# One-hot rows of the dense gates: compares on Vector and GpSimd against products of index bits on TensorE

## The chip, the cores and the metric

The kernel runs on one core of one Trainium2 chip. The metric is the device time of one launch in microseconds (us); lower is better. The engines are named as the profile names them: PE is TensorE (PEld its weight loads), DVE is VectorE, ACT is ScalarE, POOL is GpSimd and SP the queue that issues most DMAs.

## The reference, cut to what matters

The model has two layers. Each ends in an expert layer (PEER) over 16384 single-neuron experts, numbered by a pair (i, j) of 0 to 127 each:

```python
        q = (xt @ w_q).reshape(n, PEER_HEADS, 2, PEER_DHALF)
        s = jnp.einsum('nhpd,hpkd->nhpk', q, keys).astype(jnp.float32)
        sv, si = lax.top_k(s, PEER_TOPK)
        cand = sv[:, :, 0, :, None] + sv[:, :, 1, None, :]
        cidx = si[:, :, 0, :, None] * PEER_NKEYS + si[:, :, 1, None, :]
        cs, ci = lax.top_k(cand.reshape(n, PEER_HEADS, -1), PEER_TOPK)
        eidx = jnp.take_along_axis(cidx.reshape(n, PEER_HEADS, -1), ci, axis=-1)
        gate = jax.nn.softmax(cs, axis=-1)
        a = jnp.einsum('nd,nhkd->nhk', xt, u[eidx]).astype(jnp.float32)
        w = (gate * jax.nn.gelu(a, approximate=False)).astype(xt.dtype)
        return jnp.einsum('nhk,nhkd->nd', w, v[eidx])
```

There are 8 heads; each keeps its 16 best i, its 16 best j and of their sums the 16 best. So every token has 128 selected experts, each with i, j and a gate.

## The kernel before, in words

The even mixer, the first expert layer, the odd mixer and the second expert layer follow one another. In an expert layer the last 128 of the 512 latent tokens (in the first layer the 256 context tokens too) fetch their experts' rows one by one (`gather`, L998 to L1024). For the first 384 tokens, three blocks of 128, all 16384 experts are computed densely (`dense_u`, `dense_w`, `dense_v`), and a dense matrix of gates, [i, token] for each j, holds zero wherever an expert was not selected. This matrix is what the change is about.

`peer` first opens a routing stage (`route`): `scores` (L872 and the lines before it) forms the scores and the top 16 of both key sets, `select` (L936 to L989) finds a block's 128 pairs: i in `fi` (L978), j in `fj` (L969), gates in `dgt` (L989), with a token on each partition. As soon as a block's two halves are selected, `gate_build` makes its gates, while the selections of the later blocks still run. Its tiles come out of the pool of the routing stage; `alloc` hands out five buffers of 128x1024 that `select` uses.

`gate_build` before (L1044 to L1093), for a block:
- PE transposes i, j and gates (L1055), so that the 128 selected experts of a token lie on the partitions. DVE splits an index into its upper 3 and lower 4 bits (L1056 to L1059).
- The block is cut into 8 chunks of 16 tokens. For a chunk DVE compares the upper bits with 8 values and the lower bits with 16 (four `is_equal`, L1070, tiles `gup` and `glow`), and POOL multiplies the gates into one of the lower tables (L1073).
- For each four tokens of a chunk, and for i and for j, one multiply (L1084) makes the one-hot rows `ghot`, 128x512, as upper times lower. So a chunk has eight multiplies; `GENG` gives five of eight to DVE and three to POOL. Six `ghot` buffers turn.
- For each token PE multiplies the one-hot rows of i by those of j (weighted with the gate) to a 128x128 matrix (L1090, tile `gps`; the trace has two instructions for one such product). ACT copies eight tokens at a time, reordered, to `gch` (L1092), and a chunk goes to DRAM (`gd`, L1093).

After the routing stage the dense stage loads these gates (`dG`, L1139) and runs 128 steps. Beside the gate work, the routing stage already computes the first products of 18 (first layer) or 27 (second) of the 128 steps (L1112 with `whi`, `wlo`, split on ACT at L185 and on DVE or POOL at L188, loaded through SP at L182), so that PE is not idle.

PSUM is full in the routing stage: two buffers `pj`, two of two banks `big` (`gps` among them) and two of one bank `po` (used here for the transposes at L1055 and for the scores).

The order on each engine is laid down when the program is built: a planner goes through simulated time, and an engine is given work that is ready and has its buffers; what the program issues first goes first, unless `later` or `issue_after` says otherwise. On the chip each engine then keeps that order, and so does the SP queue.

Of the kernel before, what the change touches and what calls it, by code (L numbers as in the profile page):

```python
# [60 lines left out]
def _cst_layout():  # L61
    off = 0
    for name, n in (("ident", 128), ("ones", 128), ("perm", 128), ("mf", 128), ("mb", 128),
                    ("iota", 128), ("start", 16), ("cos", 512), ("sin", 512)):
        CST[name] = (off, n)
        off += n
    return off
# [5 lines left out]
def constants():  # L73
# [27 lines left out]
    put("start", np.array(starts)[None, :])  # L101
    return c


class Kern:
    def __init__(self, ctx, tc, a, dbg=None):
# [8 lines left out]
        self.wcnt, self.wlo, self.ghot = 0, WL1, 0  # L115
# [12 lines left out]
        self.yd = self.dr.tile([2, D, 768], F32, name="yd")  # L128

# [11 lines left out]
    def mixing(self):  # L141
        """pools of the parts between the expert layers"""
# [13 lines left out]
    def later(self, offset=1 << 20):  # L156
        """what is issued inside gives way to what is issued up to `offset` later"""
# [20 lines left out]
    def weight(self, src, shape):  # L178
        """src: DRAM AP of `shape` ([128, k, n], 1024 elements a row); returns (hi, lo)."""
# [11 lines left out]
    def wT(self, w, c0):  # L191
        """columns c0..c0+128 of the weights w as [128 k, 8, 128]."""
# [725 lines left out]
    def select(self, l, V, I, out, half, alloc):  # L918
# [17 lines left out]
        if fi is None:  # L936
            fi, fj = W(4, 16), W(4, 16)
# [584 lines left out]
```

## Time and profile before

| | us |
|---|---|
| median of 3 runs (lowest, highest) | 4348.12 (4344.39, 4353.43) |
| span of the profiled execution, first to last instruction | 4350.6 |
| PE busy | 3739.3 (86%) |
| DVE busy | 3715.8 (85%) |
| POOL busy | 2683.4 (62%) |
| ACT busy | 1603.3 (37%) |

The profiled execution has no other time of its own than its span, which already lies within the three runs. A page of the profile gives busy time by engine, the chain of work that ended last and the costliest groups; the views of the trace cut that to a stretch, a line or a tile. The routing stages with their gate work lie at about 1080 to 1515 us (first layer) and 2930 to 3390 us (second).

### The profile page before, as it was taken

To read this page: it belongs to the slowest core of one execution; us is meant where nothing else is said; L and a number is where in the kernel's file an instruction comes from. 1 tells how busy PE (TensorE), PEld (TensorE's weight loads), DVE (VectorE), ACT (ScalarE), POOL (GpSimd) and SP (SyncE) were. 2 spreads that over 40 slices of the span, in tenths; PEclk is the share of its full clock that TensorE was granted. 3 is DMA by queue.
4 is the path that set the end of the run, shared out by engine and by line. 5 is a ranking of instruction groups with operands and counts; after the bars stand their busy time and mean duration, and the time that the engine had idled before them with its cause. 6 is when DMAs were issued, how large, how long until landed. Compare 5 with 4: busy or idle time off the path is not lost.

```text
span 4350.6 us, 58785 instructions
## 1 busy us (share of the span) xinstructions
PE 3739.3 (86%) x20576; PEld 3297.7 (76%) x20576; DVE 3715.8 (85%) x6089; ACT 1603.3 (37%) x2676; POOL 2683.4 (62%) x1886
## 2 busy tenths in 40 slices
PE   7977666756687699999999968899886999999999
PEld 5776654445567689988889857787875899999987
DVE  6479989979999998898989989747999887777788
ACT  4433433412115533333333325443245433333333
POOL 3146777656656677777878667112577676666664
PEclk9998888878798999999999989999989999999999
DMA  5554888788742499999899988423234987887878
GB/s 192 187 185 158 276 284 280 263 308 317 241 135 109 184 337 336 332 320 327 318 331 335 341 301 290 160 84 125 94 126 168 321 309 272 285 287 269 288 264 313
DMA packets 382487, 1093.10 MB, mean 251 GB/s; under 512 B 32671, under 2 KB 134375, under 8 KB 376046
## 3 DMA queue, kind: packets, MB, share of 16 engines
q0 software_dynamic: 147456, 536.94, 34.8%
q1 hardware_dynamic: 224942, 491.58, 32.9%
q10 hardware_dynamic: 9792, 60.82, 3.4%
q8 instruction: 162, 2.65, 0.2%
q14 instruction: 135, 1.11, 0.1%
HBM read 1020.96 MB, written 68.26 MB: 250 GB/s over the span
## 4 chain that ended last, share of the span: by engine, by line
PE 40%; DVE 25%; issue 15%; DMA 11%; POOL 7%; ACT 2%; SPq 0%; POOLq 0%; DVEq 0%; ACTq 0%
PE dacc L1161 17%; PE dA L1112 14%; POOL uv L998 4%; DVE ghot L1084 4%; DMA uv<-in_pr_u_dram,ix 3%; DMA draw<-in_uT_dram 3%; DVE junkv L1011 3%; DMA uv<-in_pr_v_dram,ix 2%; PE ops L214 1%; DVE wlo L188 1%; DVE pacc L1024 1%; PE pqps L204 1%; DVE sel L916 1%; DVE gup L1070 1%; DVE sel L913 1%
## 5 line engine op out<-in xcount | busy, mean ns | idle before, releaser
L1161 PE MATMUL dacc<-dhi,dw 128*128 128x512 f32 x3072 | 989.1, 392 | 3.4 <-ACT dw L1154 1.8
L998 POOL DMA_INDIRECT uv<-in_pr_v_dram,ix x512 | 685.6, 1339 | 405.0 <-DVE pacc L1024 297.6
L998 POOL DMA_INDIRECT uv<-in_pr_u_dram,ix x512 | 685.2, 1338 | 373.6 <-DVE pa L1011 204.3
L1011 DVE CUSTOM_DVE_ANT_0 junkv<-uv,x 128x1024 bf16<-128x1024 f32 x512 | 734.7, 1435 | 39.5 <-DMA uv<-in_pr_u_dram,ix 35.5
L1024 DVE SCALAR_TENSOR_TENSOR pacc<-uv,pw,pacc 128x1024 f32<-128x1024 f32 x508 | 705.1, 1388 | 26.9 <-DMA uv<-in_pr_v_dram,ix 23.0
L1161 PEld LDWEIGHTS dacc<-dhi,dw 128*128 128x128 f32 x3072 | 579.9, 189 | 120.7 <-ACT dw L1154 2.1
L1101 ACT CAST dhi<-draw 128x1024 fp32r<-128x1024 f32 x467 | 489.2, 1050 | 463.6 <-DMA draw<-in_uT_dram 165.9
L1161 PE MATMUL dacc<-dlo,dw 128*128 128x512 f32 x1536 | 604.4, 394 | 11.1 <-DVE dlo L1102 11.0
L1102 POOL TENSOR_TENSOR dlo<-draw,dhi 128x1024 fp32r<-128x1024 f32 x210 | 545.5, 2598 | 95.6 <-ACT dhi L1101 91.9
L188 POOL TENSOR_TENSOR wlo<-wraw,whi 128x1024 fp32r<-128x1024 f32 x111 | 280.0, 2523 | 426.0 <-ACT whi L185 282.1
L1151 DVE TENSOR_TENSOR dz<-dz,dG 128x384 f32<-128x384 f32 x256 | 402.4, 1585 | 89.9 <-ACT dz L1121 88.5
L1154 ACT CAST dw<-dz 128x384 fp32r<-128x384 f32 x256 | 131.4, 513 | 690.8 <-PE dacc L1161 669.8
L1102 DVE TENSOR_TENSOR dlo<-draw,dhi 128x1024 fp32r<-128x1024 f32 x257 | 336.1, 1308 | 27.3 <-ACT dhi L1101 18.1
L185 ACT CAST whi<-wraw 128x1024 fp32r<-128x1024 f32 x195 | 204.3, 1049 | 416.6 <-PE pqps L204 101.5
L1112 PE MATMUL dA<-xth,dhi 128*128 128x384 f32 x1688 | 334.8, 340 | 10.1 <-ACT dhi L1101 6.9
L1161 PEld LDWEIGHTS dacc<-dlo,dw 128*128 128x128 f32 x1536 | 289.8, 189 | 70.1 <-DVE dlo L1102 13.3
L1112 PE MATMUL dA<-xtl,dhi 128*128 128x384 f32 x1688 | 327.4, 335 | 0.0
L1112 PEld LDWEIGHTS dA<-xth,dhi 128*128 128x128 f32 x1688 | 305.1, 189 | 28.5 <-ACT dhi L1101 7.8
L1112 PE MATMUL dA<-xth,dlo 128*128 128x384 f32 x1688 | 326.7, 334 | 0.0
L1090 PE MATMUL gps<-ghot 128*128 128x128 f32 x1536 | 231.8, 307 | 104.5 <-DVE ghot L1084 80.2
L1090 PEld LDWEIGHTS gps<-ghot 128*128 128x128 f32 x1536 | 211.2, 216 | 126.3 <-issue 84.4
L1112 PEld LDWEIGHTS dA<-xtl,dhi 128*128 128x128 f32 x1688 | 296.7, 188 | 0.0
(379 smaller groups left out, 6836.6 us busy)
## 6 DMA issues: line engine op xcount, KB each, us to landing
draw<-in_pr_v_dram SPq DMA_DIRECT2D x256, 512.0 KB
draw<-in_uT_dram SPq DMA_DIRECT2D x211, 512.0 KB
wraw<-in_wb_dram SPq DMA_DIRECT2D x150, 512.0 KB
gd<-gch ACTq DMA_DIRECT2D x48, 1024.0 KB
dG<-gd SPq DMA_DIRECT2D x30, 1536.0 KB
wraw<-in_mod_t_dram SPq DMA_DIRECT2D x48, 512.0 KB
wraw<-in_uT_dram SPq DMA_DIRECT2D x45, 512.0 KB
wraw<-in_mod_w_dram SPq DMA_DIRECT2D x32, 512.0 KB
```

What stands on the lines that cost most here:

```text
L185: nc.scalar.copy(hi, raw)
L188: eng.tensor_tensor(lo, raw, hi.bitcast(F32), op=OP.subtract)
L998: nc.gpsimd.indirect_dma_start(out=t, out_offset=None, in_=a[table], in_offset=bass.IndirectOffsetOnAxis(ap=ix[:, c:c + 1], axis=0))
L1011: nc.vector.tensor_tensor_reduce(out=junk, in0=u, in1=x, op0=OP.mult, op1=OP.add, scale=1.0, scalar=0.0, accum_out=A[:, c:c + 1])
L1024: nc.vector.scalar_tensor_tensor(acc, v, W[:, c:c + 1], acc, op0=OP.mult, op1=OP.add)
L1084: eng.tensor_tensor(h.rearrange("p t (a b) -> p t a b", b=16), up[:, e, t0:t0 + 4, :].unsqueeze(3).broadcast_to([128, 4, 8, 16]), low[:, e ...
L1090: nc.tensor.matmul(ps[:, t0 - 8 * q + t, :], hot[0][:, t, :], hot[1][:, t, :], start=True, stop=True)
L1101: nc.scalar.copy(hi, raw)
L1102: eng.tensor_tensor(lo, raw, hi.bitcast(F32), op=OP.subtract)
L1112: nc.tensor.matmul(A, u[ui][:, k, :], xt[xi][:, k, 0:ND], start=(i == 0), stop=(i == 23))
L1151: nc.vector.tensor_tensor(z3, z3, self.G[:, :, j % JG, :], op=OP.mult)
L1161: self.nc.tensor.matmul(acc[b][:, h, :], w[wi][:, 128 * b:128 * b + 128], v[vi][:, 512 * h:512 * h + 512], start=(j == 0 and i == 0), stop ...
```

## The change

The one-hot rows are no longer made by compares. Seven bit planes of i and j (each plane 0 or 2^e, e = 0 to 6) and a plane of ones go, as bf16 and with a token on a partition, to a DRAM tensor `bd` and come back with (token, plane) on the partitions and the 128 selected experts along the free axis. One product with a constant matrix `gB` ([16 tokens x 8 planes, 16 x 128 values], zero for other tokens) then gives, for four tokens and all 128 values, 1 where all bits agree and 0 or less elsewhere. ACT reads the product of i with Relu, DVE that of j with a maximum with 0 and a multiplication by the gate. POOL makes no one-hot rows any more; the products `d` take the two `po` buffers of PSUM. The rest (L1090 to L1093) stays. `fi` and `fj` become the halves of one tile `fij`; the bit planes are made in three buffers of `alloc`.

```diff
-GENG = "vpvpvvvp"           # engines that make the one-hot rows in turn: Vector, Pool
...
+    bits = (p[None, :] >> np.arange(7)[:, None]) & 1
+    coef = np.concatenate([(2.0 * bits - 1.0) / 2.0 ** np.arange(7)[:, None], 1.0 - bits.sum(0)[None, :]], 0)
+    put("coef", np.tile(coef, (16, 1)))
+    put("tmask", p[:, None] // 8 == np.arange(16)[None, :])
...
+        self.bd = self.dr.tile([ND // 128, 1024, 256], BF16, name="bd")
...
+    def gate_consts(self):
...
+        self.gB = self.wk.tile([128, 16, 128], BF16, name="gB")
+        nc.vector.tensor_tensor(self.gB, self.c("coef")[:, None, :].broadcast_to([128, 16, 128]),
+                                self.c("tmask").unsqueeze(2).broadcast_to([128, 16, 128]), op=OP.mult)
+
+    def gate_build(self, b, sel, alloc):
...
-        for n, src in enumerate((fi, fj, g)):
-            nc.tensor.transpose(pt[:, n, :], src, self.ident)
-        nc.vector.tensor_copy(cu, pt[:, 0:2, :])
-        nc.vector.tensor_scalar(cu, cu, 15, None, op0=OP.bitwise_and)
-        nc.vector.tensor_copy(cols[:, 2:4, :], cu)
-        nc.vector.tensor_tensor(cols[:, 0:2, :], pt[:, 0:2, :], cols[:, 2:4, :], op=OP.subtract)
-        nc.scalar.copy(cols[:, 4, :], pt[:, 2, :])
-        TG = 16
+        _, g, fij, _ = sel
+        pl = alloc().bitcast(BF16).rearrange("p (e x) -> p e x", e=8)
+        nc.gpsimd.memset(pl[:, 7, :], 1.0)
+        for s in range(2):
+            bu = alloc().bitcast(U32).rearrange("p (e x) -> p e x", e=8)
+            nc.vector.tensor_copy(bu[:, 7, :], fij[:, 128 * s:128 * s + 128])
+            for e in range(7):
+                nc.vector.tensor_scalar(bu[:, e, :], bu[:, 7, :], 1 << e, None, op0=OP.bitwise_and)
+            nc.vector.tensor_copy(pl[:, 0:7, 128 * s:128 * s + 128], bu[:, 0:7, :])
+        nc.sync.dma_start(self.bd[b].rearrange("(t e) x -> t e x", e=8), pl)
+        pt = self.po([128, 128], "gtp")
+        nc.tensor.transpose(pt, g, self.ident)
+        gT = wk.tile([128, 128], F32, name="gT", tag="gT", bufs=2)
+        nc.scalar.copy(gT, pt)
         for c in range(8):
...
-                for n, (t, at) in enumerate(((up, iota[:, 0:128:16]), (low, iota[:, 0:16]))):
-                    m = t.shape[-1]
-                    for e in range(2):
-                        nc.vector.tensor_tensor(
-                            t[:, e], at[:, None, :].broadcast_to([128, TG, m]),
-                            cols[:, 2 * n + e, tk].unsqueeze(2).broadcast_to([128, TG, m]), op=OP.is_equal)
-                nc.gpsimd.tensor_tensor(low[:, 1], low[:, 1],
-                                        cols[:, 4, tk].unsqueeze(2).broadcast_to([128, TG, 16]), op=OP.mult)
+            if c % 4 == 0:
+                bits = wk.tile([128, 4, 256], BF16, name="gbits", tag="gbits", bufs=2)
+                nc.sync.dma_start(bits, self.bd[b].rearrange("(c p) x -> p c x", p=128)[:, c:c + 4, :])
             G = wk.tile([128, 128, 16], F32, name="gch", tag="gch", bufs=2)
             for q in range(2):
                 ps = self.big([128, 8, 128], "gps")
                 for t0 in (8 * q, 8 * q + 4):
                     hot = []
-                    for e in range(2):
+                    for s in range(2):
+                        d = self.po([128, 4, 128], "gds")
+                        nc.tensor.matmul(d, bits[:, c % 4, 128 * s:128 * s + 128], self.gB[:, t0:t0 + 4, :],
+                                         start=True, stop=True)
                         h = wk.tile([128, 4, 128], F32, name="ghot", tag="ghot", bufs=6)
-                        eng = nc.gpsimd if GENG[self.ghot % len(GENG)] == "p" else nc.vector
-                        self.ghot += 1
-                        eng.tensor_tensor(
-                            h.rearrange("p t (a b) -> p t a b", b=16),
-                            up[:, e, t0:t0 + 4, :].unsqueeze(3).broadcast_to([128, 4, 8, 16]),
-                            low[:, e, t0:t0 + 4, :].unsqueeze(2).broadcast_to([128, 4, 8, 16]), op=OP.mult)
+                        if s == 0:
+                            nc.scalar.activation(h, d, AF.Relu)
+                        else:
+                            t = 16 * c + t0
+                            nc.vector.scalar_tensor_tensor(
+                                h, d, 0.0, gT[:, t:t + 4].unsqueeze(2).broadcast_to([128, 4, 128]),
+                                op0=OP.max, op1=OP.mult)
                         hot.append(h)
...
+                self.gate_consts()
                 sel = self.route(l, xt, nb, nd, alloc, self.gate_build)
```

`gate_consts` is called once in each layer, ahead of `route`.

## Rows read from the trace of the kernel before

**Rows 1.** Spans and clock of the core.
```profile
core 0: 4350.6 us, clock 0.933
```
**Rows 2.** The page: chain that ended last, share of the span by engine and line.
```profile
PE 40%; DVE 25%; issue 15%; DMA 11%; POOL 7%; ACT 2%; SPq 0%; POOLq 0%; DVEq 0%; ACTq 0%
```
**Rows 3.** Busy time by stretch (us): PE, PEld, DVE, ACT, POOL, clock, DMA, GB/s.
```profile
1304.00:1380.00 76.00, 57.34 (x343) 54.78 (x341) 74.91 (x128) 38.16 (x42) 50.23 (x39) 0.89 0.27 104
1380.00:1508.00 128.00, 90.34 (x595) 82.54 (x596) 121.14 (x164) 68.24 (x41) 89.96 (x69) 0.91 0.42 164
3280.00:3385.00 105.00, 68.95 (x464) 61.31 (x464) 95.78 (x125) 55.94 (x31) 70.90 (x55) 0.93 0.44 171
```
**Rows 4.** Groups by line and shape, 3280 to 3385 us: busy, mean ns | idle before.
```profile
L1084 DVE TENSOR_TENSOR ghot<-gup,glow 128x512 f32<-128x512 f32 x71 | 73.1, 1088 | 0.2 <-PE gps L1090 0.2
...
L1092 ACT COPY gch<-gps 128x1024 f32<-128x1024 f32 x30 | 57.2, 1912 | 46.3 <-PE gps L1090 45.8 <-ACT gch L1092 0.5
```
**Rows 5.** Timeline: first gate products of each layer, the end of the last ones.
```profile
1304.29 4.28 PE L1090 MATMUL gps<-ghot 128*128 128x128 f32 x24
...
1505.79 1.13 PE L1090 MATMUL gps<-ghot 128*128 128x128 f32 x8 [0.34 <-DVE ghot L1084]
1506.96 1.93 ACT L1092 COPY gch<-gps 128x1024 f32<-128x1024 f32 x1 [2.05 <-PE gps L1090]
...
1510.53 0.97 PEld L1090 LDWEIGHTS gps<-ghot 128*128 128x128 f32 x8 [0.50 <-issue]
1510.56 1.13 PE L1090 MATMUL gps<-ghot 128*128 128x128 f32 x8 [0.34 <-DVE ghot L1084]
...
3172.20 3.89 PE L1090 MATMUL gps<-ghot 128*128 128x128 f32 x24
...
3380.84 1.84 PE L1090 MATMUL gps<-ghot 128*128 128x128 f32 x15
```
**Rows 6.** Nearest rows for the two reads of a product: ACT and DVE, 128x512.
```profile
L869 ACT COPY pq<-pqps x48: 348/585/589, 260.7 to 3075.3; 128x512 f32<-128x512 f32 x32, 128x256 f32<-128x256 f32 x16
...
L714 DVE TENSOR_TENSOR rt<-rps,cst 128x512 f32<-128x512 f32 x8 | 5.5, 684 | 0.0
```
**Rows 7.** Nearest rows for the product: 512 columns on PE, issue and duration.
```profile
1104.41 1.98 PE L204 MATMUL pqps<-xth,wlo 128*128 128x512 f32 x8
...
L1161 PE MATMUL dacc<-dhi,dw 128*128 128x512 f32 x3072 | 989.1, 392 | 3.4 <-ACT dw L1154 1.8
```
**Rows 8.** Timeline: from the end of a DVE row to PE.
```profile
3339.70 1.57 DVE L1084 TENSOR_TENSOR ghot<-gup,glow 128x512 f32<-128x512 f32 x1
...
3341.39 0.97 PEld L1090 LDWEIGHTS gps<-ghot 128*128 128x128 f32 x8 [0.53 <-issue]
3341.43 1.13 PE L1090 MATMUL gps<-ghot 128*128 128x128 f32 x8 [0.37 <-DVE ghot L1084]
```
**Rows 9.** Timeline of the odd mixer: two `po` buffers between PE and ACT.
```profile
2701.24 0.75 ACT L1313 COPY opT<-opt 128x384 f32<-128x384 f32 x2 [0.17 <-PE opt L1312]
2701.77 1.38 PE L1318 MATMUL oo<-ov,opT 128*128 128x128 f32 x10 [0.21 <-ACT opT L1313]
2702.99 0.49 PE L1312 MATMUL opt<-cst,op 128*128 128x128 f32 x3
```
**Rows 10.** Selection's last j and two small integer operations on DVE.
```profile
1281.89 1.21 DVE L969 TENSOR_REDUCE fj<-sel 128x64 f32<-128x1024 f32 x1
...
3144.76 1.21 DVE L969 TENSOR_REDUCE fj<-sel 128x64 f32<-128x1024 f32 x1
...
1273.00 0.20 DVE L976 TENSOR_SCALAR sel<-sel 128x64 uint32<-128x64 uint32 x1
...
1268.04 1.22 DVE L965 TENSOR_TENSOR sel<-sel,cst 128x1024 f32<-128x1024 f32 x1
```
**Rows 11.** The chain from 3150 to 3420 us: a transfer to DRAM and back.
```profile
3384.67 3.88 DMA gd<-gch
3388.62 3.98 DMA dG<-gd
```
**Rows 12.** What the SP queue waited for, 3150 to 3300 us (total, times, longest).
```profile
SPq L182 <- POOL sel L943: 15.9, 1, 15.9
SPq L182 <- POOL wlo L188: 15.8, 3, 10.5
```
**Rows 13.** PE work of L1112 alone, by stretch: PE, PEld, clock.
```profile
1300.00:1400.00 100.00, 43.70 (x200) 37.74 (x200) 0.88 0.27 106
3165.00:3200.00 35.00, 13.67 (x57) 12.02 (x57) 0.78 0.25 90
3200.00:3290.00 90.00, 35.79 (x169) 32.13 (x168) 0.90 0.40 152
```

More of the change, by code (lines that the diff above doesn't have):

```diff
@@ L63, in _cst_layout @@
     for name, n in (("ident", 128), ("ones", 128), ("perm", 128), ("mf", 128), ("mb", 128),
-                    ("iota", 128), ("start", 16), ("cos", 512), ("sin", 512)):
+                    ("iota", 128), ("start", 16), ("cos", 512), ("sin", 512),
+                    ("coef", 128), ("tmask", 16)):
         CST[name] = (off, n)
@@ L114, in __init__ @@
         self.wk = None
-        self.wcnt, self.wlo, self.ghot = 0, WL1, 0
+        self.wcnt, self.wlo = 0, WL1
         nc = self.nc
@@ L889, in route @@
             out.append([sq(pg, "ix", 3, U32), sq(pg, "gt", 3), None, None] if b >= nd else
-                       [None] + [sq(wk, n, 3) for n in ("dgt", "fi", "fj")])
+                       [None, sq(wk, "dgt", 3), wk.tile([128, 256], F32, name="fij", tag="fij", bufs=3), None])
         pick = lambda b, half: self.select(l, V[b], I[b], out[b], half, alloc)
@@ L901, in route @@
                     if half == 1:
-                        after(b, out[b])
+                        after(b, out[b], alloc)
             for b in range(nd, nb):
@@ L933, in select @@
         V, I = V[:, hs, :], I[:, hs, :]
-        ix, g, fi, fj = (t if t is None else
-                         t[:, 64 * half:64 * half + 64].rearrange("p (h k) -> p h k", h=4) for t in out)
-        if fi is None:
-            fi, fj = W(4, 16), W(4, 16)
+        part = lambda t, o=0: t[:, o + 64 * half:o + 64 * half + 64].rearrange("p (h k) -> p h k", h=4)
+        ix, g, fij, _ = out
+        g, ix = part(g), ix if ix is None else part(ix)
+        fi, fj = (W(4, 16), W(4, 16)) if fij is None else (part(fij), part(fij, 128))
         IF = W(8, 16)
@@ L1042, in resid @@
         return h
-    def gate_build(self, b, sel):
-        nc, wk = self.nc, self.wk
-        iota = self.c("iota")
-        _, g, fi, fj = sel
-        cols = wk.tile([128, 5, 128], F32, name="gcol", tag="gcol", bufs=1)
-        cu = wk.tile([128, 2, 128], U32, name="gcu", tag="gcu", bufs=1)
-        pt = self.po([128, 3, 128], "gtp")
-        for n, src in enumerate((fi, fj, g)):
-            nc.tensor.transpose(pt[:, n, :], src, self.ident)
-        nc.vector.tensor_copy(cu, pt[:, 0:2, :])
-        nc.vector.tensor_scalar(cu, cu, 15, None, op0=OP.bitwise_and)
-        nc.vector.tensor_copy(cols[:, 2:4, :], cu)
-        nc.vector.tensor_tensor(cols[:, 0:2, :], pt[:, 0:2, :], cols[:, 2:4, :], op=OP.subtract)
-        nc.scalar.copy(cols[:, 4, :], pt[:, 2, :])
-        TG = 16
-        for c in range(8):
-            if 16 * c % TG == 0:
-                tk = slice(16 * c, 16 * c + TG)
-                up = wk.tile([128, 2, TG, 8], F32, name="gup", tag="gup", bufs=2)
-                low = wk.tile([128, 2, TG, 16], F32, name="glow", tag="glow", bufs=2)
-                for n, (t, at) in enumerate(((up, iota[:, 0:128:16]), (low, iota[:, 0:16]))):
-                    m = t.shape[-1]
-                    for e in range(2):
-                        nc.vector.tensor_tensor(
-                            t[:, e], at[:, None, :].broadcast_to([128, TG, m]),
-                            cols[:, 2 * n + e, tk].unsqueeze(2).broadcast_to([128, TG, m]), op=OP.is_equal)
-                nc.gpsimd.tensor_tensor(low[:, 1], low[:, 1],
-                                        cols[:, 4, tk].unsqueeze(2).broadcast_to([128, TG, 16]), op=OP.mult)
@@ new lines, in gate_consts @@
+    def gate_consts(self):
+        nc = self.nc
+        self.gB = self.wk.tile([128, 16, 128], BF16, name="gB")
+        nc.vector.tensor_tensor(self.gB, self.c("coef")[:, None, :].broadcast_to([128, 16, 128]),
+                                self.c("tmask").unsqueeze(2).broadcast_to([128, 16, 128]), op=OP.mult)
+    def gate_build(self, b, sel, alloc):
+        nc, wk = self.nc, self.wk
+        _, g, fij, _ = sel
[12 more added lines that the diff above has]
+        nc.scalar.copy(gT, pt)
+        for c in range(8):
+            if c % 4 == 0:
+                bits = wk.tile([128, 4, 256], BF16, name="gbits", tag="gbits", bufs=2)
+                nc.sync.dma_start(bits, self.bd[b].rearrange("(c p) x -> p c x", p=128)[:, c:c + 4, :])
```

## The prediction

> **What bounds the kernel now.** I read the core's line first, then the chain, then the stretches with gate work, and only there groups and single rows. The profiled execution spans 4350.6 us [rows 1], 2.5 us above the median of the three runs (4348.1). The sum is made against its own span, and its difference is put on the median. In the chain PE leads with 40% and DVE has 25% [rows 2]: an average over stages with different limits. The change touches only the routing stages, so what counts is who is full there. In the three stretches DVE is busy for 74.9 of 76, 121.1 of 128 and 95.8 of 105 us, and ACT for about half [rows 3]. In the last stretch PE ran 464 instructions, all of them gate products; at 32 to a chunk of 16 tokens that is 14.5 chunks, in the 103 us up to the last of them: 7.1 us a chunk. There DVE spends 73.1 us on 71 one-hot multiplies, 1088 ns each, while ACT waits 45.8 us for PE [rows 4]. So DVE (with POOL, which shares the multiplies) sets the pace. Over a whole layer the gate products run from 1304.3 to 1511.7 and from 3172.2 to 3382.7 us [rows 5]: 207 and 210 us for 24 chunks, 8.7 us a chunk, more than 7.1 because in the first half the later blocks' selections have their share of DVE. **The change wins if a chunk, all hindrance counted, takes under 8.7 us.**
>
> **The change, part by part.** *Removed*, for each chunk: five multiplies and four compares on DVE, three multiplies and one more on POOL. That is the present bound, whole.
>
> *Added*, for each chunk: eight products on PE, four Relu reads on ACT, four reads on DVE. No row shows exactly these. A read of 128x512 from PSUM took 585 ns on ACT (a copy) and 684 ns on DVE (two operands, one in PSUM) [rows 6]; I take these. A product of 512 columns: eight issue in 1.98 us, 0.25 us each, and one takes 392 ns to its result [rows 7]; these are of another type, so I allow half as the lower end of the issue time. Gate products stay at 0.97 us for eight instructions (four tokens) [rows 8].
>
> *Engine sums for a chunk*: PE 4 x 0.97 + 8 x 0.25 = 5.9 us; ACT 4 x 0.585 + 2 x 1.91 (the copy to gch, [rows 4]) = 6.2; DVE 4 x 0.684 = 2.7; POOL nothing. If everything overlapped, a chunk would take 6.2 us.
>
> *What need not overlap*: the products go into two PSUM buffers, and four tokens need both, one for i (read by ACT) and one for j (read by DVE). DVE's read of the j product does two things as it ends: it makes this group's gate products ready, and it frees the buffer for the next group's j product. If PE takes the older work first, it runs the four gate products (0.97 us), then the next j product; its result comes 0.39 us later, is picked up 0.04 us after that (PE ends at 1506.92, ACT starts at 1506.96 [rows 5]), DVE reads for 0.68 us, and PE starts 0.16 us after DVE's end (3341.27 to 3341.43 [rows 8]). That is a ring in which PE and DVE wait for each other: 0.97 + 0.39 + 0.04 + 0.68 + 0.16 = 2.24 us for four tokens, 9.0 us a chunk. The i product and ACT's read fit beside it. The ends are 6.2 (all overlaps) and 10.0 (the next i product, 0.25 us, also goes ahead of the j product in each of the four). I take 9.0, since where PE and ACT share the same two buffers in the odd mixer PE does take the older work first: it runs ten older products from 2701.77 and three younger transposes only at 2702.99, though ACT had emptied a buffer by 2701.99 [rows 9].
>
> *The start*: block 0 has its last j at 1283.1 and 3146.0 us [rows 10]. Bit planes: for i and for j one copy (0.2 us), seven small operations (0.2 each) and a cast of 896 values, which I put at 1.05 us (1024 took 1.22): 2 x 2.65 = 5.3 us [rows 10], and 2 us for other work on DVE between them. Out to DRAM and back: 3.9 + 4.0 us [rows 11], for larger transfers, so an upper end; the lower is perhaps half. With 1.3 us for a first group (0.39 + 0.04 + 0.68 + 0.16) the gate products begin at about 1299.6 and 3162.5, 5 and 10 us earlier than now.
>
> *Hindrance*: while the later selections, bit planes and weight splits still use DVE, a j read can find an operation running, the long ones 1.2 us [rows 10]. That concerns some ten chunks, 40 reads: 0 to 48 us a layer. I take 0.35 us a read, 14 us, since DVE is free two thirds of a ring.
>
> *The buffers of alloc*: bit planes take three of five, two are held by the routing, so the selection of block 1 starts later by the planes' 5.3 us and their write. Cover: the 72 us of block 0's eight chunks. Were it gone, some 10 us.
>
> *SP*: a block adds one write and two reads to SP's queue, in order behind weight loads that wait for buffers, up to 15.9 us at once [rows 12]. Only block 0's first transfer is uncovered: 0 to 16 us a layer. I take 0 (the planner knows these waits) and make the rest a rival. Behind a waiting bits transfer stand weight loads for the first products, which have until the end of the stage.
>
> *Smaller*: gB costs DVE two times 1.22 us a layer [rows 10], before the first scores are there; 2.4 us if that cover is gone. The 144 more columns of constants and the fewer transposes I set at nothing.
>
> *Sum*: first layer -5 + 24 x 9.0 + 14 - 207 = +18; second -10 + 216 + 14 - 210 = +10. The dense stages follow and move as they are: **+28 us**, 4379 against the span, **4376** against the median. A measurement of this kernel can tell about 0.2% (9 us) from no change.
>
> **Rivals.** *1. PE runs ahead (faster).* If PE gets the next j product ahead of the gate products, the read hides under them and the pace is that of the engines. PE then also has the first products of the dense steps to do, 200 weight loads in the first layer (37.7 us) and 226 in the second (44 us) [rows 13], which today fill its gaps. First layer 24 x 5.9 + 38 = 180 us from 1299.6, an end at 1480, -32 us; second 142 + 44 from 3162.5, an end at 3348.5, -34: together -66, 4282 us. Between the two, at 8.0 us a chunk, it is 28 - 48 = -20, 4328 us. It decides at 8.3 to 8.6 us a chunk without hindrance ((207 + 5 - 14) / 24 and (210 + 10 - 14) / 24). For it: all engine sums lie below 6.2. Against: only two buffers, and rows 9. The Trainium skill (Perfetto Trace Analysis, section Matmuls) says that independent matmul groups should rotate through PSUM banks so that the evacuation of one overlaps the next group's matmuls; by that rule the two products, each with a bank of its own, would reach this rival's time. Chance 0.30, for all of it between -66 and -10 us.
>
> *2. Late bits (slower still).* SP's head waits for a weight buffer while block 0's planes or bits are due: 16 us a layer [rows 12], +28 + 32 = +60, 4408 us. For it: the waits of today; against: the planner places transfers by its own time. Chance 0.14.
>
> *3. It cancels.* At 8.4 us a chunk the sum is zero: the change takes work off DVE and POOL that the stage then spends on the ring, 4348 us. Chance 0.10.
>
> **How the numbers follow.** The forecast has 0.46; its own range is 4355 to 4400 (8.6 to 9.5 us a chunk). Of it 0.34 lies above +0.2%, 0.09 within and 0.03 below. Rival 1 gives 0.28 to faster and 0.02 to the same, rival 2 0.14 to slower, rival 3 0.10 to the same: faster 0.31, same 0.21, slower 0.48. The range must take in a partial overlap below and rival 2 or a ring of 10.0 us (+48, 4424) above: 4295 to 4425. It leaves out the full overlap at its best and several mishaps at once, some 0.15.
>
> **What would show it.** Right: in the stretch after the selections PE's gate products come in eights about 2.2 us apart, the wait ahead of each put down to DVE's ghot, with one product d right behind each eight and DVE under 40% busy; the first gate product of a layer at about 1300 and 3162; reads of 0.58 and 0.68 us on ACT and DVE. Wrong: both products d ahead of an eight and a pace of 6 to 7 us a chunk (rival 1); SP waits of over 10 us ahead of bd or gbits and a first gate product after 1310 (rival 2); reads much longer than those of rows 6, for then the ring has another length; or a dense stage that does not simply move.

## The result, and the profile after

The changed kernel takes 4403.08 us (median of 4 runs, 4401.25 to 4408.99) where the kernel before takes 4346.26 (4 runs): a ratio of 1.0128, with a 95% interval of 1.0109 to 1.0146. **It is slower by 1.3%, twice what was forecast** (+57 us between the medians; +28 was forecast). The time lies just above the forecast's own range (4355 to 4400) and inside the whole one (4295 to 4425). Between the two profiled executions it is 4399.4 against 4350.6 us, +48.8; the rest is that one span lies above its median and the other below it. The accounts that follow are those of the spans.

The core's line, then the page's chain, to be held beside [rows 1] and [rows 2]:

```profile
core 0: 4399.4 us, clock 0.939
...
PE 47%; DVE 21%; issue 13%; DMA 10%; POOL 7%; ACT 2%; SPq 0%; POOLq 0%; DVEq 0%; ACTq 0%
```

DVE's share of the chain fell by 4 points and PE's rose by 7. The stretches of [rows 3], in the same columns:

```profile
1304.00:1380.00 76.00, 62.68 (x351) 53.55 (x349) 59.90 (x180) 42.51 (x62) 27.49 (x27) 0.91 0.25 96
1380.00:1508.00 128.00, 99.12 (x596) 64.65 (x597) 40.83 (x59) 87.17 (x92) 0.00 (x0) 1.00 0.35 140
3280.00:3385.00 105.00, 80.84 (x487) 52.39 (x484) 33.91 (x49) 71.61 (x75) 0.00 (x0) 1.00 0.34 137
```

In the last two, DVE fell from 121.1 and 95.8 to 40.8 and 33.9 us and POOL from 90.0 and 70.9 to nothing, as the change says. Yet no engine is full there: PE has 77%, ACT 68%, and the DMA engines stand at 0.35 and 0.34. **Where no engine is full, waits set the pace; here they close to a ring.** The groups of the third stretch, which answer to [rows 4] (busy, mean ns | idle before, and what ended it):

```profile
L1100 PE MATMUL gps<-ghot 128*128 128x128 f32 x387 | 56.1, 287 | 22.6 <-DVE ghot L1095 22.6
L1102 ACT COPY gch<-gps 128x1024 f32<-128x1024 f32 x25 | 47.5, 1898 | 22.2 <-PE gps L1100 22.2
...
L1095 DVE SCALAR_TENSOR_TENSOR ghot<-gds,gT 128x512 f32<-128x512 f32 x49 | 33.9, 692 | 72.1 <-PE gds L1088 72.1
L1088 PE MATMUL gds<-gB,gbits 128*128 128x512 bf16 x98 | 32.9, 378 | 1.5 <-ACT gT L1076 0.7
L1092 ACT ACTIVATE ghot<-gds 128x512 f32<-128x512 f32 x48 | 29.7, 618 | 11.1 <-PE gds L1088 11.1
```

PE waits for DVE's read (22.6 us) and DVE waits for PE's product (72.1 us): each for the other. The timeline from 1503 us shows the links (start, duration, engine):

```profile
1503.20 1.16 PE L1100 MATMUL gps<-ghot 128*128 128x128 f32 x8 [0.38 <-DVE ghot L1095]
1504.09 0.21 PEld L1088 LDWEIGHTS <-gbits 128*128 128x128 bf16 x2
1504.19 0.59 PE L1088 MATMUL gds<-gB,gbits 128*128 128x512 bf16 x2
1504.39 1.90 ACT L1102 COPY gch<-gps 128x1024 f32<-128x1024 f32 x1 [0.94 <-PE gps L1100]
1504.61 0.69 DVE L1095 SCALAR_TENSOR_TENSOR ghot<-gds,gT 128x512 f32<-128x512 f32 x1 [1.47 <-PE gds L1088]
1505.36 0.97 PEld L1100 LDWEIGHTS gps<-ghot 128*128 128x128 f32 x8 [1.06 <-DVE ghot L1095]
1505.36 1.16 PE L1100 MATMUL gps<-ghot 128*128 128x128 f32 x8 [0.57 <-DVE ghot L1095]
```

An eight (the eight instructions of four tokens' gate products) starts at 1503.20, the products d follow at 1504.19 (0.99 later), DVE's read at 1504.61 (0.42), the next eight at 1505.36 (0.75): 2.16 us for four tokens, 8.6 us a chunk. The stage as a whole is slower than that, though. For both layers, the line of the gate products (ns min/median/max, first and last start), before and after, and that of dacc, the second products of the dense stage, in the first layer:

```profile
L1090 PE MATMUL gps<-ghot x768: 271/275/554, 1304.3 to 1511.4; 128*128 128x128 f32 x192
L1161 PE MATMUL dacc<-dhi,dw x1536: 386/389/632, 1525.1 to 2528.2; 128*128 128x512 f32 x192
L1090 PE MATMUL gps<-ghot x768: 269/275/554, 3172.2 to 3382.4; 128*128 128x128 f32 x192
```

```profile
L1100 PE MATMUL gps<-ghot x768: 270/275/582, 1288.0 to 1543.0; 128*128 128x128 f32 x192
L1171 PE MATMUL dacc<-dhi,dw x1536: 387/389/632, 1557.2 to 2543.9; 128*128 128x512 f32 x192
L1100 PE MATMUL gps<-ghot x768: 270/275/542, 3177.1 to 3431.3; 128*128 128x128 f32 x192
```

| stretch | before | after | difference |
|---|---|---|---|
| start to the first gate product, first layer | 1304.3 | 1288.0 | -16.3 |
| gate products, first layer | 207.1 | 255.0 | +47.9 |
| to the last dense product, first layer | 1016.8 | 1000.9 | -15.9 |
| to the first gate product, second layer | 644.0 | 633.2 | -10.8 |
| gate products, second layer | 210.2 | 254.2 | +44.0 |
| to the end of the span | 968.2 | 968.1 | -0.1 |

So 92 us are lost in the two gate stages and 43 come back elsewhere. At 8.6 us a chunk 24 chunks are 207 us, not 255. Where the other 48 us of the first layer go, the gate products alone show, by stretch (us, PE busy and instructions, 32 to a chunk, clock, DMA, GB/s):

```profile
1288.00:1360.00 72.00, 13.35 (x89) 0.93 0.26 95
1400.00:1500.00 100.00, 53.57 (x373) 1.00 0.35 139
```

From 1400 on it is 373 instructions in 100 us, 8.6 us a chunk. In the first 72 us it is 89, **26 us a chunk, while selections of other blocks and the first products dA of the dense steps (L1122) run beside it**. The experiments take these two apart: the ring, and what slows the first 72 us.

### The profile page after: what moved, and what is told of

Its sections match the earlier page's. It is cut to its first block, busy times and chain, and to the rows that moved or that the text cites. A ratio compares the mean times of both kernels' runs of the same rounds, so it can differ in the third digit from the quotient of the medians.

```text
span 4399.4 us, 59129 instructions
## 1 busy us (share of the span) xinstructions
PE 3815.3 (87%) x20948; PEld 3292.4 (75%) x20948; DVE 3528.4 (80%) x5935; ACT 1703.6 (39%) x2868; POOL 2440.6 (55%) x1700
## 4 chain that ended last, share of the span: by engine, by line
PE 47%; DVE 21%; issue 13%; DMA 10%; POOL 7%; ACT 2%; SPq 0%; POOLq 0%; DVEq 0%; ACTq 0%
PE dacc L1171 16%; PE dA L1122 15%; POOL uv L1005 5%; PE gps L1100 4%; DVE ghot L1095 3%; DMA uv<-in_pr_u_dram,ix 3%; DMA draw<-in_uT_dram 2%; DVE junkv L1018 2%; DMA uv<-in_pr_v_dram,ix 2%; PE pqps L211 2%; PE ops L221 1%; DVE wlo L195 1%; PE modps L252 1%; DVE pacc L1031 1%; DVE sel L923 1%
## 5 line engine op out<-in xcount | busy, mean ns | idle before, releaser
L1112 POOL TENSOR_TENSOR dlo<-draw,dhi 128x1024 fp32r<-128x1024 f32 x210 | 544.9, 2596 | 439.3 <-ACT dhi L1111 435.8
L1018 DVE CUSTOM_DVE_ANT_0 junkv<-uv,x 128x1024 bf16<-128x1024 f32 x512 | 723.2, 1413 | 42.8 <-DMA uv<-in_pr_u_dram,ix 38.9
L195 POOL TENSOR_TENSOR wlo<-wraw,whi 128x1024 fp32r<-128x1024 f32 x111 | 277.7, 2502 | 432.5 <-ACT whi L192 231.5
L1112 DVE TENSOR_TENSOR dlo<-draw,dhi 128x1024 fp32r<-128x1024 f32 x257 | 338.9, 1319 | 22.6 <-ACT dhi L1111 14.8
L1100 PEld LDWEIGHTS gps<-ghot 128*128 128x128 f32 x1536 | 190.6, 194 | 200.9 <-DVE ghot L1095 198.1
L1122 PE MATMUL dA<-xth,dhi 128*128 128x384 f32 x1688 | 334.2, 340 | 7.4 <-ACT dhi L1111 6.8
L1095 DVE SCALAR_TENSOR_TENSOR ghot<-gds,gT 128x512 f32<-128x512 f32 x192 | 132.5, 690 | 248.4 <-PE gds L1088 248.4
L1122 PE MATMUL dA<-xtl,dhi 128*128 128x384 f32 x1688 | 328.3, 335 | 0.0
L1122 PE MATMUL dA<-xth,dlo 128*128 128x384 f32 x1688 | 326.5, 334 | 0.0
L1122 PEld LDWEIGHTS dA<-xth,dhi 128*128 128x128 f32 x1688 | 305.3, 189 | 24.4 <-ACT dhi L1111 7.2
```

Source lines behind the costliest of these rows:

```text
L195: eng.tensor_tensor(lo, raw, hi.bitcast(F32), op=OP.subtract)
L1018: nc.vector.tensor_tensor_reduce(out=junk, in0=u, in1=x, op0=OP.mult, op1=OP.add, scale=1.0, scalar=0.0, accum_out=A[:, c:c + 1])
L1095: nc.vector.scalar_tensor_tensor(h, d, 0.0, gT[:, t:t + 4].unsqueeze(2).broadcast_to([128, 4, 128]), op0=OP.max, op1=OP.mult)
L1100: nc.tensor.matmul(ps[:, t0 - 8 * q + t, :], hot[0][:, t, :], hot[1][:, t, :], start=True, stop=True)
L1112: eng.tensor_tensor(lo, raw, hi.bitcast(F32), op=OP.subtract)
L1122: nc.tensor.matmul(A, u[ui][:, k, :], xt[xi][:, k, 0:ND], start=(i == 0), stop=(i == 23))
```

## The experiments

All changes are made in `gate_build` of the changed kernel if nothing else is said. Ratios are against the kernel before.

**1. The next group's products ahead.** In `gate_build` the two products d and the two reads of a group stand ahead of the gate products of the group before it; two banks as now.

```diff
+        hot = prod(0)
+        for k in range(32):
+            nxt = prod(k + 1) if k < 31 else None
...
+            for t in range(4):
+                nc.tensor.matmul(ps[:, t0 % 8 + t, :], hot[0][:, t, :], hot[1][:, t, :], start=True, stop=True)
...
+            hot = nxt
```

> The two index-bit products of the next four tokens and their two reads are issued ahead of the gate products of this group; the same two product banks, the whole computation. Ring theory (TensorE takes older gate products before younger index-bit products, so that each group pays product, read, gate products one after the other: 2.16 us per four tokens, 8.6 us per chunk in the trace of the changed kernel): after the last selection step (about 1360 and 3248 us) the products stand in their banks while TensorE does gate products, the pace drops to 6 to 8 us per chunk, and the gate stage ends 15 to 50 us earlier in each layer: total 4300 to 4370 us. Rival, the pace is set by two banks that ScalarE and Vector must hand back (each held for product plus read, whatever the order): pace stays at 8.3 to 8.7 us per chunk, total 4390 to 4410 us. Hindrance theory (before 1360 us the pace is set by reads that stand in Vector's queue behind selection work): the stretch up to 1360 us makes 2.5 to 4 chunks as now.

Measured: 4351.3 us, ratio 0.9997 (0.9984 to 1.0010); the pace is 432 instructions in 100 us, 7.4 us a chunk, and the stages take 226.4 and 228.3 us. The order alone gives the loss back, but not the 6 us a chunk: the timeline shows the ring on the other side now.

```profile
1442.21 0.33 ACTq L1114 DMA_DIRECT2D gd<-gch  x1
1442.58 0.60 ACT L1091 ACTIVATE ghot<-gds 128x512 f32<-128x512 f32 x1
1442.66 0.38 PE L1087 MATMUL gds<-gB,gbits 128*128 128x512 bf16 x1 [0.74 <-ACT ghot L1091]
...
1442.87 1.05 PE L1109 MATMUL gps<-ghot 128*128 128x128 f32 x8
```

PE's next product waits 0.74 us for a bank that ACT's Relu hands back; ACT had a copy of 1.89 us (from 1440.29) in front of its reads. The first 72 us are slow as before (104 instructions of gate products by 1360, for 89).

**2. Four banks.** A tag of its own, two banks, for the product of j; to make room the gate products come out of one-bank tiles of four tokens, with a copy for each.

```diff
-                ps = self.big([128, 8, 128], "gps")
...
+                    ps = self.ps.tile([128, 4, 128], F32, name="gps", tag="gps1", bufs=2)
...
-                        d = self.po([128, 4, 128], "gds")
+                        d = (self.po([128, 4, 128], "gds") if s == 0 else
+                             self.ps.tile([128, 4, 128], F32, name="gdj", tag="gdj", bufs=2))
```

> Two banks more for the index-bit products (the gate products come out of one-bank tiles with a copy of 4 tokens each), order of the program as in the changed kernel, the whole computation. Ring theory, in the form that the two banks tie the products of one group to the reads of the last: the products run a group ahead, pace 6.2 to 7 us per chunk after the selections, the gate stage ends 35 to 50 us earlier per layer, total 4300 to 4335 us. Rival, that the order of the program (older gate products first) alone ties them: pace stays 8.3 to 8.7 us per chunk plus what the second copy of 4 tokens costs ScalarE, total 4390 to 4420 us. Before 1360 us no change (2.5 to 4 chunks) if Vector's queue sets that pace.

Measured: 4271.14 us, ratio 0.9812 (0.9791 to 0.9833): **132 us below the changed kernel and 1.9% below the kernel before.** It went further than expected, since the first 72 us sped up too, where I had expected no change:

```profile
1288.00:1360.00 72.00, 20.41 (x144) 0.98 0.35 126
1400.00:1460.00 60.00, 45.27 (x329) 1.00 0.54 209
```

329 instructions in 60 us are 5.8 us a chunk, and 144 against 89 came out by 1360. From 1400 to 1460 PE is busy for 57.5 and ACT for 57.1 of the 60 us: two engines are nearly full. The stage takes 189.5 and 187.9 us.

**3. Both together** (the order of 1 with the banks of 2).

> Both edits: two banks more and the products of the next group issued ahead. Ring theory: pace 6 to 6.6 us per chunk after the selections (TensorE busy without gaps, 48 products at 0.29 us or weight loads at 0.19 us beside it), total 4290 to 4325 us and below the kernel before. Rival (ScalarE: 4 reads of 0.6 us and four copies of a chunk come to about 6.5 us, or the reads of one group wait for the bank of the last): 7.5 to 8.7 us per chunk, total 4360 to 4410 us.

Measured: 4270.35 us, ratio 0.9805 (0.9784 to 0.9827). With a bank pair for each reader the order adds nothing that can be measured: this ring needs both, two banks and that order, to close.

**4. The control for 2**: one-bank gate tiles and small copies alone, both products still in the `po` pair.

> Control for the run with four product banks: only the second half of that edit. Gate products come out of one-bank tiles of four tokens with a copy of 512 each; the index-bit products keep their two banks. The whole computation. Bank theory (two product banks tie a group's products to its own reads): the eights of gate products stay 2.1 to 2.3 us apart after the selections, total 4385 to 4410 us. Rival (the long copy on ScalarE was what held the ring, or the gate tiles were): pace falls toward 6 us a chunk, total below 4330 us.

Measured: 4394.68 us, ratio 1.0102 (1.0085 to 1.0119), and the eights stand at the old distance:

```profile
1441.74 1.16 PE L1100 MATMUL gps<-ghot 128*128 128x128 f32 x8 [0.57 <-DVE ghot L1095]
...
1443.89 1.16 PE L1100 MATMUL gps<-ghot 128*128 128x128 f32 x8 [0.57 <-DVE ghot L1095]
```

2.15 us apart. So it is the banks of the products that brought the gain of 2.

**5. DVE out of the ring.** The product of j is read by ACT with Relu too; the factor of the gate value is left out.

```diff
-                        if s == 0:
+                        if True:
                             nc.scalar.activation(h, d, AF.Relu)
```

> The second index-bit product is read by ScalarE with Relu as the first is; the factor by the gate value is left out of the computation. Vector has no part in the gate stage. Hindrance theory (the first chunks are slow because each read waits in Vector's queue behind selection work): the pace from 1288 us on is set by ScalarE and the ring, 8.6 to 10 us per chunk from the first chunk on, and the 32 groups of a layer end by 1365 to 1375 us for chunks one to eight of the first block; the gate stage ends 25 to 45 us earlier in each layer, total 4320 to 4360 us. Rival, the first chunks are slow by the round trip of the bits through device memory or by other work that TensorE puts ahead: still under 4 chunks by 1360 us, and total 4390 to 4430 us since ScalarE's eight reads a chunk and its copies come one after the other.

Measured: 4613.8 us, ratio 1.0591 (1.0564 to 1.0619). Both sides of the expectation failed, by 254 and by 184 us above their upper ends. I had added up ACT's work (8.6 us a chunk) and left out that it would now be in the ring: both reads and the copy stand one after the other between two eights, and in ACT's order nothing else can run while it waits. PE's waits of 2 us are followed by eights that take up to 2.08 instead of 1.16 us, with a granted clock of 0.84 from 1400 to 1500:

```profile
1440.66 1.17 ACT L1092 ACTIVATE ghot<-gds 128x512 f32<-128x512 f32 x2
1440.82 0.38 PE L1088 MATMUL gds<-gB,gbits 128*128 128x512 bf16 x1 [1.95 <-ACT ghot L1092]
1441.30 1.78 PEld L1100 LDWEIGHTS gps<-ghot 128*128 128x128 f32 x8 [2.71 <-ACT ghot L1092]
1441.30 2.08 PE L1100 MATMUL gps<-ghot 128*128 128x128 f32 x8
```

As a test of the first 72 us it decides nothing: they are slow here too, but ACT's queue has waits for selection work of its own.

**6. The value of the early start.** All planes and gates are asked for behind all selections.

```diff
-                    if half == 1:
-                        after(b, out[b], alloc)
...
+            for b in range(nd):
+                after(b, out[b], alloc)
```

> As the changed kernel, but all planes and gates are asked for behind the selections of all four blocks. It prices what the early start is worth: in the changed kernel 2.8 chunks come out by 1360 us. Queue theory (selections and gate stage hold each other up while they overlap): the selections end 8 to 15 us earlier without reads and planes between them, the gate stage then runs at 8.6 us a chunk from its first chunk, 207 us, and ends within 15 us of now: total 4390 to 4430 us. Rival (the early chunks cost the selections nothing): the selections end within 4 us of now, the gate stage ends 20 to 30 us later per layer, total 4440 to 4465 us.

Measured: 4433.1 us, one run, between what the two sides expected. The selections end no earlier (the last ix at 1360.8, against 1360.2), as the rival had it, and the stage stands almost alone (22 and 65 instructions of dA at its start):

```profile
L1100 PE MATMUL gps<-ghot x768: 270/275/377, 1354.8 to 1564.1; 128*128 128x128 f32 x192
L1100 PE MATMUL gps<-ghot x768: 270/275/377, 3247.2 to 3462.2; 128*128 128x128 f32 x192
```

209.3 and 215.0 us for 24 chunks, 8.7 and 9.0 each: **this is the ring nearly undisturbed, where the forecast has 24 x 9.0 = 216.** Starting 67 and 70 us earlier, as the changed kernel does, brings the end forward by only 21 and 31 us; the other 46 and 39 us are what the overlap costs the gates.

**7. TensorE's filler.** Of the products dA in the routing stage one of three terms is computed, the others are left out; loads and splits stay.

> Of the first products of the experts that are done ahead in the routing stage (dA, 18 and 27 of them) only one of three terms is computed: two thirds of that TensorE work are left out of the computation, while their weight loads, the splits on ScalarE, Vector and GpSimd stay. Queue theory (the first chunks are slow because each read of a product stands behind selection work, bit planes and splits in the in-order queue of Vector, or of ScalarE): the stretch from 1288 to 1360 us makes 70 to 110 gate instructions as in the changed kernel (89), and the gate stage ends within 10 us of 1543 us. Rival, TensorE's own queue (24 dA products, 4.1 us, between a product and its gate products): over 150 gate instructions by 1360 us, the gate stage ends 20 us or more earlier in each layer, total 4345 to 4370 us.

**8. Less of it**: 2 of 24 products of each dA, the other 22 left out.

> As the run with one of three dA terms, but only 2 of the 24 dA products of each expert that is done ahead in the routing stage are computed; the other 22 are left out of the computation, their loads and splits stay. If the time that TensorE gives to dA accounts for what remained there, the gate stage falls from 230 and 235 us to 212 to 222 us in each layer; if what remains are reads that stand behind work in the queues of Vector and ScalarE, it stays at 226 to 235 us.

**9. None of it**: dA left out whole in the routing stage.

```diff
-                    z[j] = self.dense_u(j, u, self.pj([128, ND], "dA"), xt)
+                    z[j] = self.dz.tile([128, ND], F32, name="dz", tag="dz", bufs=self.upre + 1)
+                    nc.scalar.copy(z[j], self.cst[:, 0:ND])
```

> As the changed kernel, but none of the dA products of the routing stage is computed (left out of the computation; weight loads, splits and ScalarE's copy stay), so that TensorE's in-order queue holds gate work alone from the first gate product on. With 2 of 24 left, the gate stage took 230 and 231 us, and in its trace dA products that wait for their splits stand ahead of index-bit products. If the place in TensorE's order is what remains, the gate stage falls to 209 to 220 us in each layer, with the first gate product at 1288 to 1300 us. If reads behind work in the queues of Vector and ScalarE remain, it stays at 222 to 235 us.

Measured (one run each): 4366.4, 4375.1 and 4386.5 us. Their gate lines in the first layer, in that order:

```profile
L1100 PE MATMUL gps<-ghot x768: 270/275/583, 1298.6 to 1528.7; 128*128 128x128 f32 x192
```

```profile
L1100 PE MATMUL gps<-ghot x768: 270/275/582, 1298.5 to 1528.4; 128*128 128x128 f32 x192
```

```profile
L1100 PE MATMUL gps<-ghot x768: 270/276/583, 1298.8 to 1532.5; 128*128 128x128 f32 x192
```

230.1, 229.9 and 233.7 us where the changed kernel has 255.0 (second layer 235.4, 231.5 and 233.1 for 254.2). In the first layer stage and selections both move back by 10 us or more (the last ix at 1371.4, 1373.8 and 1375.7), so they overlap for 73 to 77 us, for 72. By what was expected, 7 speaks for TensorE's queue (168 gate instructions by 1360 us), 8 and 9 for the reads. But the three are nearly one test: in 7 already only 24 instructions of dA stand between 1298 and 1360 us, where the changed kernel has 202. Without dA the stage is about 20 to 25 us shorter, so **of the 46 and 39 us the products dA, standing in TensorE's order between a product d and its gate products, cost about half**, perhaps more, since the clock fell in all three. What remains in 9 is not the products dA. There, where TensorE's queue holds hardly anything but gates, PE's own list of waits between 1300 and 1360 us names the reads (us in total, times, longest):

```profile
PE gds L1088 <- ACT ghot L1092: 14.4, 11, 2.0
PE gps L1100 <- DVE ghot L1095: 3.9, 5, 1.2
```

And an emptier PE loses clock: granted are 0.84, 0.83 and 0.72 from 1298 to 1375 us in 7, 8 and 9, against 0.91 in the changed kernel. How the rest divides between reads that stand behind other work and the lower clock, these runs do not settle.

**10. Cheaper planes.** One cast and seven operations on 16 bits a block put the bits in place; the constants of `coef` become `bits - 0.5`.

```diff
-        for s in range(2):
...
+        bu = alloc().bitcast(mybir.dt.uint16)[:, 0:256]
+        nc.vector.tensor_copy(bu, fij)
+        for e in range(7):
+            nc.vector.tensor_scalar(pl.bitcast(mybir.dt.uint16)[:, e, :], bu, 1 << e, 14 - e,
+                                    op0=OP.bitwise_and, op1=OP.logical_shift_left)
```

> The bit planes of a block come from one cast and seven operations on 128x256 of 16 bits that write the bits in place, instead of two casts in, fourteen operations and two casts out: Vector's work for a block falls from 5.5 us unstretched (and 8 to 13 us where GpSimd runs beside it) to about 2 to 3 us. The whole computation, order otherwise as in the changed kernel. Queue theory with the planes as its main part: the first bits leave 3 to 5 us earlier, the selections of the other blocks end 6 to 12 us earlier in each layer, the gate stage 8 to 20 us earlier, total 4365 to 4390 us. Rival (the planes are only a small part of what the reads wait for, or others' work takes their place): total 4392 to 4405 us, the same as the changed kernel.

Measured: 4396.4 us, ratio 1.0089 (1.0071 to 1.0108), inside the rival's range; that interval ends just below the changed kernel's (1.0109 to 1.0146), so a few us may be real. The planes of all blocks cost DVE 15.9 us now (3.2 + 12.7), where the changed kernel spends 44.3 (5.2 + 26.4 + 12.7), and the selections end 7 us earlier (the last ix at 1353.2), but the gate stages end at 1538.0 and 3430.8, 5 and 0.5 us earlier. DVE's saving hardly reaches the end of the stage; what takes it up was not followed.

**11. Banks and planes together.**

> Two banks more for the products and the cheap bit planes together; the whole computation. If the two effects add: 4271 less 10 to 30 us, 4240 to 4262 us. If the selections are no longer what the stage waits for once the products have four banks: 4265 to 4273 us.

Measured: 4266.83 us, ratio 0.9792 (0.9774 to 0.9810). It can't be told from 2.

**12. Then a copy from ACT to DVE.**

```diff
+                    cp = nc.vector.tensor_copy if b > 0 and t0 == 8 else nc.scalar.copy
+                    cp(G[:, :, t0:t0 + 4].rearrange("p j t -> p t j"), ps)
```

> The kernel with four product banks and cheap bit planes, where for the second and third block one of a chunk's four copies of gate products goes from ScalarE to Vector; the whole computation. With four banks ScalarE is full (18.4 to 19.8 of 20 us) and Vector is at 8 to 10 of 20. If ScalarE sets the pace there: 5.75 falls to about 5.2 us a chunk over 16 chunks, 8 us less in each layer, total 4245 to 4262 us. If TensorE or the order on the queues does: no change, 4262 to 4280 us.

Measured: 4260.82 us, ratio 0.9801 (0.9783 to 0.9819). The pace is 362 instructions in 60 us, 5.3 us a chunk, and now PE is full (the stretch, columns as in rows 3):

```profile
1400.00:1460.00 60.00, 60.00 (x454) 52.27 (x453) 40.71 (x57) 55.16 (x82) 0.00 (x0) 1.00 0.66 248
```

In the trace the stages are 5.9 and 5.6 us shorter than in 11 (179.8 and 182.5 us for 185.7 and 188.1); the ratios of 2, 3, 11 and 12 don't tell the four versions apart. All of them beat both kernels, by about 2% and 3%.

## Why the prediction was right, and which term was mis-sized

**What bounds.** DVE did set the pace before, and it was set free: 31.8 us of 100 from 1400 on. The forecast's reason for a loss nevertheless, a ring in place of a full engine, is what the trace shows.

**The ring: right.** Forecast 0.97 + 0.39 + 0.04 + 0.68 + 0.16 = 2.24 us; measured 0.99 + 0.42 + 0.75 = 2.16. The eight and the product are as taken; DVE's read is 0.69 and PE starts only 0.06 after its end, not 0.16. Reads of 0.62 us on ACT and 0.69 on DVE stand against 0.585 and 0.684 of [rows 6]. Its cause was tested from both sides: the order undone (1), the banks doubled (2), and the control (4). The Trainium skill (Perfetto Trace Analysis, section Matmuls) was weighed in the prediction as a rule by which separate banks alone would let reads and products overlap: the runs agree with the rule once each of the two products has a pair of banks, 8.6 against 5.8 us a chunk, and show that one bank for each was not enough here.

**Rival 1 (PE runs ahead): false for the change, right for the edit of experiment 2.** Its bounds, 180 and 186 us for a gate stage, are near what four banks gave (189.5 and 187.9).

**The start: planes and transfer near, the first group and the starting point not.** In the first layer the planes take 6.4 us from block 0's last j (1268.0) to the write of bd (1274.4), where 7.3 was forecast; the way through DRAM 8.7 us, to the first product d at 1283.1, for 7.9; the first group 4.9, to 1288.0, for 1.3, since its read stands on DVE behind a reduction that waits for POOL. In the second layer they are 5.9, 8.0 and 5.8. In the first layer the forecast also counted from the wrong row: the j of 1281.89 [rows 10] is the second block's. Block 0's is the one ahead of it, which PE had already transposed by then (kernel before):

```profile
1274.97 1.21 DVE L969 TENSOR_REDUCE fj<-sel 128x64 f32<-128x1024 f32 x1
...
1278.86 0.27 PE L1055 MATMUL gtp<-cst,fj 128*128 128x128 f32 x1
```

From 1276.2 the same sum gives 1292.7 instead of 1299.6. The rest is that block 0's last j itself came earlier: by 8.2 us in the first layer, and by 7.3 in the second, where it stands at 3157.4, 11.4 us later than before, but the scores ahead of it end 18.7 later (3094.0 for 3075.3). Nothing in the forecast provided for that. The selections have another order: the second block's first reduction stood ahead of that j (1269.18 and 3141.66) and now stands behind it (1285.42 and 3175.25). Whether the planes' hold on the buffers of alloc brings this about was not tried.

**Rival 2 (late bits): false.** 8.7 and 8.0 us from the write to the first product leave no room for SP waits of 16.

**Rival 3 (cancels): false.** Against its 8.4 us a chunk and the sum's 14 us of hindrance stand 8.7 and 9.0 us a chunk and 46 and 39 us of hindrance (experiment 6).

**Hindrance: the term that was mis-sized.** "I take 0.35 us a read, 14 us, since DVE is free two thirds of a ring" was a price for a read that finds DVE occupied. Measured it is 46 and 39 us (experiment 6), near the upper end that I gave and then left. Two things were left out. First, TensorE: the forecast counted the products dA under rival 1 alone, as work "which today fill its gaps". The gaps of a ring are 0.4 to 0.6 us long, and PE's part is a link of it, so 24 products of 0.36 us each (eight in a row take 1.55) between a product d and its gate products lengthen the ring, however idle PE is on average. From 1288 to 1360 us PE spends 46.1 us on dA and 13.4 on gate products. Second, in-order queues: a read waits behind all that its engine has been given earlier, not behind one operation. The timeline of the changed kernel, a product of j on PE, the read of a product of i on ACT, then DVE and POOL:

```profile
1314.19 0.38 PE L1088 MATMUL gds<-gB,gbits 128*128 128x512 bf16 x1
...
1315.53 0.60 ACT L1092 ACTIVATE ghot<-gds 128x512 f32<-128x512 f32 x1 [2.06 <-PE gds L1088]
...
1315.66 5.42 DVE L1070 TENSOR_SCALAR sel<-sel 128x128 uint32<-128x128 uint32 x7
1321.00 1.21 DVE L195 TENSOR_TENSOR wlo<-wraw,whi 128x1024 fp32r<-128x1024 f32 x1
1322.13 1.07 DVE L1071 CAST sel<-sel 128x896 bf16<-128x896 uint32 x1
1323.13 0.68 DVE L1095 SCALAR_TENSOR_TENSOR ghot<-gds,gT 128x512 f32<-128x512 f32 x1
...
1315.89 2.51 POOL L975 TENSOR_TENSOR sel<-sel 128x1024 f32<-128x1024 f32 x1 [2.06 <-DVE sel L972]
1318.36 2.37 POOL L195 TENSOR_TENSOR wlo<-wraw,whi 128x1024 fp32r<-128x1024 f32 x1
```

The product of j was issued at 1314.19; its read came 8.9 us later, behind a compare, seven plane operations, a split and a cast. (The product after it, at 1315.11, is one of i: ACT read it at 1315.53.)

**The sum.** Forecast +18 and +10. Measured -16.3 + 47.9 = +31.6 for the first layer; for the second +44.0, less 13.8 by which its gate products begin earlier, measured from the scores (18.7 - 4.9), +30.2. **"The dense stages move as they are" was wrong by 16 us in the first layer**: 986.7 us of dacc instead of 1003.1, and 978 to 996 us in all twelve experiments. The second moved as it was (946.5 for 946.0). In the first the DMA engines are at 0.93 in both kernels and move the same (329 GB/s for 1003 us, 335 for 987). PE's idle time fell from 15.0 to 5.9 us, its waits for dlo (the low half of the split weights, from DVE) from 10.1 to 5.3 between 1600 and 2500; its busy time fell from 988.0 to 981.1 at a granted clock of 0.99 and 1.00. Why was not tried and stays open, and with one profile of each kernel it is not shown that the 1003 us recur. Without those 16 us the time would have been about 4419, near the upper end of the range.

**Luck.** Of the 21 us by which the spans' +48.8 passes the forecast's +28, hindrance alone is 57 too little; the start (15), the first dense stage (16) and the ring (8) erred the other way, and 3 us more came between the layers. That the time lies in the range is owed in part to these.

**alloc, gB.** No cost of the buffers of alloc can be seen: the last ix stands at 1360.2 and 3247.7, where it stood at 1379.9 and 3245.8 (the second behind scores that end 18.7 us later). gB takes 2.28 us a layer, where 2.44 was set down, ahead of the first scores.

## What to carry to other kernels

When a busy engine is relieved by handing its work along a chain of engines, add up the chain for one group, not each engine: with as many buffers as one group needs, the chain's length is the pace, and a pair of buffers for each hand-over opens it (8.6 to 5.8 us a chunk here, for no new work). A ring has no room for filler: work that an average of busy time calls hidden goes into the ring when it sits in the same in-order queue, so price an overlapped stretch by what stands between two links on each queue. And a control that makes half of an edit is worth its run: it showed which half had brought the gain.

## What the runs showed of the hardware that I had not expected

Small operations on DVE take many times their length while POOL works on SBUF. The line of the plane operations (ns min/median/max) says it:

```profile
L1070 DVE TENSOR_SCALAR sel<-sel x84: 211/218/2433, 1269.3 to 3215.0; 128x128 uint32<-128x128 uint32 x84
```

In the timeline above, seven of them take 5.42 us beside two POOL operations of 2.51 and 2.37 us; at 1299.72, beside short ones, seven took 1.40. The Trainium skill (SBUF — State Buffer, section Who interferes with whom) has the pair of ports that DVE, in its two-port modes, shares with GpSimd as an exclusive lock: the second to come waits for the whole instruction. The rows agree: the longest of 84 is as long as a whole POOL operation on 1024 elements. DVE's reads from PSUM never show it (192 of them, 662 to 693 ns), nor do the casts of 896 elements (1064 to 1086 ns). Making the planes with half as many operations (experiment 10) saved DVE time but did not end the waiting: their mean was still 369 ns for a minimum of 210.

That relieving TensorE can cost it its clock was the other surprise: in experiments 5 and 9 it waits up to 2 us at a time for reads, the granted clock falls to 0.84 (1400 to 1500 us) and 0.73 (1300 to 1360), and some eights of gate products there take 2.08 us instead of 1.16, as at the lower of its two levels (1.2 for 2.4 GHz). The ring is then longer, and the next wait too.
